# A 46,610-instruction transformer kernel: cross attention in a fixed order with other products between its steps, silu of the conditions kept in DRAM, index scores and root spreads a step later

## The chip, the cores and the metric

The kernel runs on one core of a Trainium2 chip. The metric is the device time of one execution in microseconds (us); smaller is better. Engine names: PE is TensorE (matmuls, weight loads are PEld), DVE is VectorE, ACT is ScalarE, POOL is GpSimd, SP is SyncE, which here only issues the transfers of weights.

## The reference, cut to what matters

Two blocks over a sequence of 256 rows of width 1024, all in fp32. The first block has two layers, each of a mixer (three kinds of attention, one of them with an index that selects keys), a cross attention to a memory of 256 rows, and a feed-forward network (FFN). The second has two layers over the latent rows and 256 rows of context, in which every norm is modulated by vectors that a condition gives.

```
def memory_cross_attention(hn, mem_n, w_q, w_kv, w_o):
    b, s, _ = hn.shape
    m = mem_n.shape[1]
    q = (hn @ w_q).reshape(b, s, H_X, HEAD_DIM)
    kv = (mem_n @ w_kv).reshape(b, m, 2, H_X, HEAD_DIM)
    sc = jnp.einsum('bqhd,bmhd->bhqm', q, kv[:, :, 0]).astype(jnp.float32) * HEAD_DIM ** -0.5
    p = jax.nn.softmax(sc, axis=-1).astype(hn.dtype)
    o = jnp.einsum('bhqm,bmhd->bqhd', p, kv[:, :, 1]).reshape(b, s, H_X * HEAD_DIM)
    return o @ w_o
...
        x = x + memory_cross_attention(rmsnorm(x, norm_cross[l]), mem_n, w_q_x[l], w_kv_x[l], w_o_x[l])
        x = x + swiglu(rmsnorm(x, norm_ffn[l]), w_gu[l], w_down[l])
...
def modulate(x, gain, shift, scale):
    return rms_norm(x, gain) * (1 + scale) + shift
...
        mod_l = (jax.nn.silu(c) @ w_mod[i] + b_mod[i]).reshape(b, N_MOD, 1, D_MODEL)
        mod_c = (jax.nn.silu(c_ctx) @ w_mod[i] + b_mod[i]).reshape(N_MOD, 1, D_MODEL)
...
    h = jnp.sin(freq * (h @ fw3 + fb3))
    h = (h @ fw4).astype(jnp.float32)
...
    h_fwd = h[:, :HY_WIDTH] * window
    h_bwd = h[:, HY_WIDTH:] * window
```

## The kernel before

Activations lie feature-major: x is [128 partitions, 8 chunks, rows], for the second block 512 columns wide, of which columns 0 to 255 are stream s=0 (latent rows) and 256 to 511 stream s=1 (context). Each fp32 product with a weight is made of three fp32r products (`mm3`, L300 to L302): high part by high part (`hh`, `whi`), low by high (`hl`, `whi`), high by low (`hh`, `wlo`). "A product" below is one of the three, 128x128 by 256 columns, unless a width is given. A weight tile of 128x1024 comes through SP's queue into one of four `raw` buffers; ACT casts it to `whi` (L195) and DVE makes `wlo` (L196). PSUM has two tags of four banks each, `acc` (products) and `aux` (everything else).

A main generator issues the products of the model in order; side generators (attention, index, norms) are advanced one step at each `yield` of the main one, so that the number of yields sets how many products stand between two steps. A scheduler then orders every engine's instructions by its own estimate of when inputs are ready. Each engine runs its list in order, so what stands in a list behind a waiting instruction waits too.

`cross(l)` makes q (tile `xq`, L905, on ACT), then for two pairs of heads: `scores` (L442; row maxima on DVE L450 and L454, exp on ACT L455 into `e`), `normalise` (DVE, L464 to L474), `flip` (transposes on PE, L489, copied by ACT to `pt`, L491), `values` (L501, split into `xoh` and `xol`, L308 and L309), then the products with w_o. Between its steps it advances a `fill`: for l = 0 keys and values of the memory for layer 1 (`mem_kv(1)`, tiles `xk1`, `xv1`), for l = 1 hyena's filter (`hyena_filter`: products with `w4` in two halves t, L1525 and L1526; DVE multiplies by a window to `hf` and `hb` and forms `hs`, L1529 to L1532; DFT products L1538 from `hs`).

`mods` makes the modulation vectors in the background, on DVE, from tiles `mraw` of w_mod and a broadcast `cb` of both conditions (1 MB, loaded five times; L1186), to which silu is applied each time (L1190 on ACT, L1191 on DVE). `norm2` makes the norms of the second block: sums of squares (`ssq`, L1281), the root on POOL (`nrs2`), a spread over the partitions (L1289), and `modulate`, for each of 8 chunks k: DVE L1290, ACT L1312, ACT L308 (`hh2`), DVE L309 (`hl2`). `fm2_split` starts a part with s=0 in an order with k outermost over four tiles of weights (96 products, 12 for each k), then s=1 tile by tile (24 products each, 3 for each k):

```
            if wide and not last:
                for k in range(KC):
                    for (wh, wl), p in zip(ws, ps):
                        self.mm3(p[:, ts], (wh[:, k], wl[:, k]), (xh[:, k, ts], xl[:, k, ts]), k == 0, k == KC - 1)
                    if k % 2:
                        yield
```

## Time and profile before

| | |
|---|---|
| Time, median of 3 runs | 2919.56 us (2919.30 to 2922.55) |
| Profiled execution: its own time, its span | 2920.18 us, 2918.4 us |
| PE busy | 2879.8 us (99%) |
| DVE, ACT, POOL busy | 2016.0 (69%), 1279.5 (44%), 73.2 us (3%) |
| Mean granted clock of PE | 0.994 of full speed |
| Transfers | 452.03 MB, 155 GB/s over the span |

The span is what the trace covers; the execution's own time has 1.8 us more. [...] A wait is put down to the instruction that released it ("<-").

### The profile page before, as it was taken

The numbers are of one execution on the slowest core, as the hardware profiler recorded it, in microseconds if no ns is written. First come the engines' busy times: TensorE is split into PE (matmuls) and PEld (weight loads), VectorE is DVE, ScalarE is ACT, GpSimd is POOL, SyncE is SP. The second block draws the span as 40 slices with busy tenths as digits, with TensorE's granted clock in tenths as the row PEclk, the third lists the DMA queues.
The fourth block names the chain that finished last, engine by engine and source line by source line (L and its number), as shares of the span: only waits on it lengthen the run. The fifth ranks groups of instructions, "written<-read, shape, count | busy, mean of one in ns | idle before, by whom it ended". The sixth has DMA issues, their size and how long they took to land.

```text
span 2918.4 us, 46610 instructions
## 1 busy us (share of the span) xinstructions
PE 2879.8 (99%) x18228; PEld 2535.0 (87%) x18228; DVE 2016.0 (69%) x3915; ACT 1279.5 (44%) x2017; POOL 73.2 (3%) x135
## 2 busy tenths in 40 slices
PE   8999999999999999999999999999999999999999
PEld 8899899989979988888977888888888889977999
DVE  7767798876878788875657656565787846535655
ACT  6665644577654542222425532123322225423543
POOL 0000000000000000000011000000000000000000
PEclk9999999999989999999999999999999999999999
DMA  7555577655546746564322234443465524522554
GB/s 228 161 162 165 176 232 237 187 155 161 181 157 208 223 147 188 185 182 124 105 67 80 88 118 146 144 148 102 139 190 184 183 92 136 164 72 87 160 185 147
DMA packets 150685, 452.03 MB, mean 155 GB/s; under 512 B 17151, under 2 KB 24872, under 8 KB 149696
## 3 DMA queue, kind: packets, MB, share of 16 engines
q1 hardware_dynamic: 147040, 435.94, 47.7%
q0 software_dynamic: 3280, 12.94, 1.4%
q8 instruction: 143, 2.34, 0.3%
q14 instruction: 78, 0.64, 0.1%
q10 hardware_dynamic: 144, 0.16, 0.0%
HBM read 447.93 MB, written 1.05 MB: 154 GB/s over the span
## 4 chain that ended last, share of the span: by engine, by line
PE 90%; issue 4%; DVE 3%; ACT 2%; DMA 1%; POOL 1%; POOLq 0%; ACTq 0%; DVEq 0%
PE acc L300 25%; PE acc L302 25%; PE acc L301 25%; PE acc L418 3%; PE acc L419 3%; PE acc L420 3%; PE aux L1857 1%; PE aux L442 1%; DVE wlo L196 1%; PE aux L489 1%; PE aux L501 1%; ACT whi L195 1%; PE aux L1552 0%; PE aux L1850 0%; PE aux L1569 0%
## 5 line engine op out<-in xcount | busy, mean ns | idle before, releaser
L195 ACT CAST whi<-raw 128x1024 fp32r<-128x1024 f32 x674 | 705.3, 1049 | 1334.9 <-PE acc L301 602.9
L300 PE MATMUL acc<-hh,whi 128*128 128x256 f32 (+1 forms) x3728 | 1174.7, 316 | 5.2 <-ACT hh L308 3.0
L196 DVE TENSOR_TENSOR wlo<-raw,whi 128x1024 fp32r<-128x1024 f32 x674 | 823.0, 1223 | 513.0 <-ACT whi L195 506.2
L302 PE MATMUL acc<-hh,wlo 128*128 128x256 f32 (+1 forms) x3728 | 1169.4, 314 | 0.1
L301 PE MATMUL acc<-hl,whi 128*128 128x256 f32 (+1 forms) x3728 | 1166.8, 313 | 0.2
L300 PEld LDWEIGHTS acc<-hh,whi 128*128 128x128 f32 x3728 | 701.0, 189 | 64.0 <-issue 8.7
L301 PEld LDWEIGHTS acc<-hl,whi 128*128 128x128 f32 x3728 | 703.3, 189 | 51.3 <-DVE hl L309 1.0
L302 PEld LDWEIGHTS acc<-hh,wlo 128*128 128x128 f32 x3728 | 702.2, 189 | 49.1 <-issue 0.4
L1200 DVE CUSTOM_DVE_ANT_0 mjunk<-mraw,cb 128x512 f32<-128x512 f32 x576 | 396.7, 689 | 26.8 <-DMA mraw<-w_mod 15.5
L300 PE MATMUL acc<-hidh,whi 128*128 128x256 f32 (+1 forms) x1152 | 373.3, 324 | 0.0
L302 PE MATMUL acc<-hidh,wlo 128*128 128x256 f32 (+1 forms) x1152 | 373.2, 324 | 0.0
L301 PE MATMUL acc<-hidl,whi 128*128 128x256 f32 (+1 forms) x1152 | 372.9, 324 | 0.0
L301 PEld LDWEIGHTS acc<-hidl,whi 128*128 128x128 f32 x1152 | 216.9, 188 | 20.0
L300 PEld LDWEIGHTS acc<-hidh,whi 128*128 128x128 f32 x1152 | 216.9, 188 | 20.0
L302 PEld LDWEIGHTS acc<-hidh,wlo 128*128 128x128 f32 x1152 | 216.9, 188 | 19.8
L418 PE MATMUL acc<-whi,hh 128*128 128x512 f32 x320 | 131.8, 412 | 0.0
L420 PE MATMUL acc<-wlo,hh 128*128 128x512 f32 x320 | 127.0, 397 | 0.0
L419 PE MATMUL acc<-whi,hl 128*128 128x512 f32 x320 | 126.6, 396 | 0.0
L1387 DVE TENSOR_TENSOR u<-acc,u 128x512 f32<-128x512 f32 (+1 forms) x88 | 55.0, 625 | 82.5 <-PE acc L302 81.8
L1367 DVE SCALAR_TENSOR_TENSOR x<-acc,modT,x 128x256 f32<-128x256 f32 x136 | 59.8, 478 | 49.3 <-PE acc L302 49.2
L418 PEld LDWEIGHTS acc<-whi,hh 128*128 128x128 f32 x320 | 60.2, 188 | 16.6 <-issue 3.5
L419 PEld LDWEIGHTS acc<-whi,hl 128*128 128x128 f32 x320 | 60.3, 188 | 14.7 <-issue 1.4
(368 smaller groups left out, 2651.6 us busy)
## 6 DMA issues: line engine op xcount, KB each, us to landing
mraw<-w_mod SPq DMA_DIRECT2D x288, 256.0 KB, 3.1
raw<-w_in SPq DMA_DIRECT2D x126, 512.0 KB, 3.6
raw<-w_gu SPq DMA_DIRECT2D x88, 512.0 KB, 4.2
raw<-ffn_a_in SPq DMA_DIRECT2D x88, 512.0 KB, 3.5
raw<-ffn_b_in SPq DMA_DIRECT2D x88, 512.0 KB, 3.5
raw<-ret_in SPq DMA_DIRECT2D x48, 512.0 KB, 3.5
raw<-w_down SPq DMA_DIRECT2D x44, 512.0 KB, 3.9
raw<-ffn_a_out SPq DMA_DIRECT2D x44, 512.0 KB, 3.5
```

The lines of the kernel that those rows point to most:

```text
L195: nc.scalar.copy(hi, raw)
L196: nc.vector.tensor_sub(lo, raw, hi.bitcast(F32))
L300: nc.tensor.matmul(out, wh, xh, start=first, stop=False)
L301: nc.tensor.matmul(out, wh, xl, start=False, stop=False)
L302: nc.tensor.matmul(out, wl, xh, start=False, stop=last)
L418: nc.tensor.matmul(o, xh[:, k, ts], wh[:, kk], start=first, stop=False)
L419: nc.tensor.matmul(o, xl[:, k, ts], wh[:, kk], start=False, stop=False)
L420: nc.tensor.matmul(o, xh[:, k, ts], wl[:, kk], start=False, stop=last)
L442: nc.tensor.matmul(banks[h][:, off[t]], pr.q[s, t * P:(t + 1) * P], pr.k[s, :nk], start=True, stop=True)
L1200: self.tc.keep_in_program_order(nc.vector.tensor_tensor_reduce(junk, w, cb[:, s, k * 512:(k + 1) * 512], 1.0, 0.0, ALU.mult, ALU.add, accu ...
L1367: nc.vector.scalar_tensor_tensor(xm, ps[:, ts], gate[:, s, m:m + 1], xm, ALU.mult, ALU.add)
L1387: nc.vector.tensor_tensor(u, pb, u, ALU.mult)
```

## The change

- `silu_c` makes silu of both conditions once, from a load `cc` at the start of the program, and writes it to DRAM; `mods` broadcasts that, and has no silu of its own.
- `cross` advances the fill once ahead of the products for q and again behind them, and then runs a written order of steps. `mem_kv(1)` and the filter yield at other places, the filter takes `acc` banks in place of `aux`. A small exp on a tile of ones stands behind q in the code, whose result nobody reads.
- `values_diff` issues its three products before the squares on them.
- `index` and `norm2` have one more `yield`.

```
         nc = self.nc
         k, v = self.xk[l], self.xv[l]
-        ps = self.fm_first([("w_kv", l, 0), ("w_kv", l, 1)], self.mem)
         if l == 0:
+            ps = self.fm_first([("w_kv", l, 0), ("w_kv", l, 1)], self.mem)
             self.mrs = self.norm_a(self.mpool)
+            yield
         else:
             for c in range(2):
-                nc.vector.tensor_tensor(k[:, c], ps[c], self.mrsb, ALU.mult)
-        yield
+                ps, = self.fm_first([("w_kv", l, c)], self.mem)
+                nc.vector.tensor_tensor(k[:, c], ps, self.mrsb, ALU.mult)
+                yield
...
+    def silu_c(self):
+
+        nc = self.nc
+        t = self.small.tile([P, 16], F32, name="ccs")
+        nc.scalar.activation(t, self.cc, AF.Sigmoid)
+        nc.vector.tensor_tensor(t, t, self.cc, ALU.mult)
+        self.silu = self.dram.tile([P, 16], F32, name="silu")
+        nc.gpsimd.dma_start(self.silu, t)
...
                 fill = self.hyena_filter()
+                next(fill)
+            ps = self.fm_first([("w_q", l, 0), ("w_q", l, 1)], (self.hh, self.hl))
+            q = mp.tile([P, 2, T], F32, name="xq")
+            for c in range(2):
+                nc.scalar.activation(q[:, c], ps[c], AF.Copy, scale=0.125)
+
+            nc.scalar.activation(self.small.tile([P, 1], F32, tag="exp0", name="exp0", bufs=1), self.ones, AF.Exp)
+            rs = self.norm_a()
+            yield
+            next(fill, None)
+            yield
...
-            for i, _ in enumerate(self.attention(pairs, lambda p: True)):
-                if i:
+            p0, p1 = pairs
+            for step in (lambda: (self.scores(p0), self.scores(p1)), None, None, lambda: (self.normalise(p0), self.flip(p0)),
+                         lambda: self.normalise(p1), None, lambda: self.flip(p1), lambda: self.values(p0), None, lambda: self.values(p1)):
+                if step:
+                    step()
+                else:
                     next(fill, None)
                 yield
...
+        if self.stop != "block1":
+            self.cc = self.small.tile([P, 16], F32, name="cc")
+            nc.gpsimd.dma_start(self.cc, bass.AP(tensor=a["cc"].tensor, offset=0, ap=[[16, P], [1, 16]]))
         lv = lt.tile([P, 2, 2, 2, 64], F32, name="lamv")
         nc.gpsimd.dma_start(lv, bass.AP(tensor=a["lamv"].tensor, offset=0, ap=[[0, P], [1, 512]]))
...
-        nc.gpsimd.dma_start(cb, bass.AP(tensor=a["cc"].tensor, offset=0, ap=[[0, P], [1, 2 * D]]))
+        nc.gpsimd.dma_start(cb.rearrange("p s d -> p (s d)"), self.silu.rearrange("(o p) k -> o (p k)", o=1).to_broadcast([P, 2 * D]))
         junk = pool.tile([P, D // 2], F32, name="mjunk")
-        for s in range(4):
-            c = cb[:, s // 2, (s % 2) * 512:(s % 2) * 512 + 512]
-            nc.scalar.activation(junk, c, AF.Sigmoid)
-            nc.vector.tensor_tensor(c, c, junk, ALU.mult)
...
         self.rsqrt(rs, v)
+        yield
         yield
...
-                pf, pb = self.aux(), self.aux()
+                pf, pb = self.acc(), self.acc()
...
-                    ps = self.aux()
+                    ps = self.acc()
```

Three places of the compiled order follow; line numbers differ by 3 to 27 between the two kernels (L905 is L927 after the change, L1289 is L1314).

ACT in the first cross attention, before: `mjunk<-cb` is the silu of the conditions, `whi` the cast of a weight tile, `e,sum` the exponentials.

```order
L1190 ACTIVATE mjunk<-cb 128x512
L195 CAST whi<-raw 128x1024 x2
L905 ACTIVATE xq<-acc 128x256 x2
L1190 ACTIVATE mjunk<-cb 128x512 x2
L455 ACT_TABLE_LOAD
L455 ACTIVATE e,sum<-aux,m,nrs 128x256 x7
L195 CAST whi<-raw 128x1024
L455 ACTIVATE e,sum<-aux,m,nrs 128x256
```

After the change, from the same two casts on:

```order
L195 CAST whi<-raw 128x1024 x2
L927 ACTIVATE xq<-acc 128x256 x2
L195 CAST whi<-raw 128x1024
L455 ACT_TABLE_LOAD
L455 ACTIVATE e,sum<-aux,m,nrs 128x256 x8
L195 CAST whi<-raw 128x1024 x2
```

The silu has left the list at this place, q follows the casts directly, and all eight exponentials stand together. The two small exps on ones, the sigmoid of `silu_c` and a table load for each of the two functions stand at the very start of ACT's list, ahead of the first high part of the memory (L312); on DVE the product of `silu_c` stands behind the two instructions on `lamv` (L1116, L1118), which already stood at its start, and all three are ahead of the first low part.

PE in the second cross attention, before, from the sums of squares behind the products for q; `sh` is the filter's hidden layer, the numbers tell tiles apart.

```order
L362 MATMUL aux_9795<-ones_70,ssq1_9793 128x1 x2
L442 MATMUL aux_9814<-xk1_88,xq_9790 128x256
...
L1525 MATMUL aux_9868<-w4_9861,sh_9194 128x512
L1526 MATMUL aux_9869<-w4_9861,sh_9194 128x512
L489 MATMUL aux_9884<-ident_69,e_9813 128x128
...
L1525 MATMUL aux_9898<-w4_9861,sh_9194 128x512
L1526 MATMUL aux_9899<-w4_9861,sh_9194 128x512
...
L1538 MATMUL aux_9921<-hs_9867,dft_9863 128x512
...
L489 MATMUL aux_9932<-ident_69,e_9834 128x128 x4
L1538 MATMUL aux_9939<-hs_9867,dft_9863 128x512 x2
```

After the change:

```order
L362 MATMUL aux_9822<-ones_72,ssq1_9820 128x1 x2
L1551 MATMUL acc_9829<-w4_9746,sh_9197 128x512
L1552 MATMUL acc_9830<-w4_9746,sh_9197 128x512
L442 MATMUL aux_9843<-xk1_90,xq_9815 128x256
...
L1551 MATMUL acc_9883<-w4_9746,sh_9197 128x512
L1552 MATMUL acc_9884<-w4_9746,sh_9197 128x512
L1564 MATMUL acc_9893<-hs_9752,dft_9748 128x512
L1564 MATMUL acc_9923<-hs_9752,dft_9748 128x512
L1564 MATMUL acc_9948<-hs_9752,dft_9748 128x512
L1564 MATMUL acc_9959<-hs_9752,dft_9748 128x512
L1564 MATMUL acc_9893<-hs_9752,dft_9748 128x512
L1564 MATMUL acc_9923<-hs_9752,dft_9748 128x512
L489 MATMUL aux_9903<-ident_71,e_9842 128x128 x4
```

The first half of the products with `w4` stands ahead of the scores, the second behind them, and six DFT products, four of them for t = 0 alone, ahead of the transposes.

DVE at this place after the change, behind the two low parts of weights; `m` are the row maxima:

```order
L1555 TENSOR_TENSOR hf<-acc,win 128x512
L1556 TENSOR_TENSOR hb<-acc,win 128x512
L450 TENSOR_REDUCE m<-aux 128x1
L1557 TENSOR_TENSOR hs<-hf,hb 128x512
L1558 TENSOR_TENSOR hs<-hf,hb 128x512
...
L1555 TENSOR_TENSOR hf<-acc,win 128x512
...
L1556 TENSOR_TENSOR hb<-acc,win 128x512
...
L450 TENSOR_REDUCE m<-aux 128x1 x2
...
L450 TENSOR_REDUCE m<-aux 128x1
L1557 TENSOR_TENSOR hs<-hf,hb 128x512
L454 TENSOR_SCALAR m<-m,nrs 128x1
L1558 TENSOR_TENSOR hs<-hf,hb 128x512
```

The second `hf`, `hb` and both second `hs` now stand among the row maxima, ahead of every `e<-e,rsum`; before, they stood behind the maxima and among those.

PE at the start of the even mixer before, `hidh2` being the end of the FFN ahead of it, `hh2` the new part's input:

```order
L1281 MATMUL aux_15227<-ones_70,ssq0_15085 128x1 x2
...
L1289 MATMUL aux_15264<-ident_69,nrs2_15231 128x128 x2
...
L300 MATMUL acc_15447<-hh2_9808,whi_15258 128x256
...
L1281 MATMUL aux_15415<-ones_70,ssq1_15083 128x1 x2
...
L1289 MATMUL aux_15475<-ident_69,nrs2_15419 128x128 x2
L300 MATMUL acc_15448<-hh2_9808,whi_15333 128x256
```

After the change:

```order
L1305 MATMUL aux_15216<-ones_72,ssq0_15074 128x1 x2
...
L1314 MATMUL aux_15283<-ident_71,nrs2_15220 128x128 x2
...
L300 MATMUL acc_15436<-hh2_9737,whi_15247 128x256
...
L1305 MATMUL aux_15404<-ones_72,ssq1_15072 128x1 x2
...
L1314 MATMUL aux_15488<-ident_71,nrs2_15408 128x128 x2
L300 MATMUL acc_15437<-hh2_9737,whi_15277 128x256
```

By the numbers of the rows 10 products stood between the first sums (`ssq0`) and their spread, and now 34; the spread for s=1 stood 51 products behind the first one that reads `hh2` (45 of s=0 left), and now 63 (33 left). Between `ssq1` and its spread stand 4 products, as before.

## Rows read from the trace of the kernel before

**Rows 1.** The page, part 1: busy time, share of the span, instructions.

```profile
PE 2879.8 (99%) x18228; PEld 2535.0 (87%) x18228; DVE 2016.0 (69%) x3915; ACT 1279.5 (44%) x2017; POOL 73.2 (3%) x135
```

**Rows 2.** Waits of PE over the span: us in total, times, longest.

```profile
PE aux L442 <- ACT xq L905: 4.9, 2, 3.3
PE aux L1525 <- ACT e L455: 3.0, 1, 3.0
PE aux L1289 <- POOL nrs L341: 2.8, 5, 1.0
PE aux L871 <- DVE ixt L728: 2.4, 2, 1.4
PE aux L521 <- ACT bo L522: 1.6, 2, 0.8
```

**Rows 3.** Timeline of ACT, first cross attention: start, duration, instruction, idle before.

```profile
309.23 0.63 ACT L1190 ACTIVATE mjunk<-cb 128x512 f32<-128x512 f32 x1 [6.61 <-DMA cb<-cc]
...
311.64 0.65 ACT L905 ACTIVATE xq<-acc 128x256 f32<-128x256 f32 x2
...
315.13 1.28 ACT L455 ACT_TABLE_LOAD   x1 [0.69 <-DVE m L454]
316.43 0.56 ACT L455 ACTIVATE e<-aux,m,nrs 128x256 f32<-128x256 f32 x1
```

**Rows 4.** Timeline of PE, first cross attention: its beginning, then the first FFN products.

```profile
305.92 0.50 PE L362 MATMUL aux<-ones,ssq 128*128 128x1 f32 x4
...
336.49 0.28 PE L300 MATMUL acc<-hh,whi 128*128 128x256 f32 x1
...
336.84 0.28 PE L300 MATMUL acc<-hh,whi 128*128 128x256 f32 x1
```

**Rows 5.** Stretches: us, busy PE, PEld, DVE, ACT, POOL; PEclk; DMA share; GB/s.

```profile
310.80:317.60 6.80, 5.53 (x24) 4.36 (x25) 6.02 (x14) 5.09 (x11) 0.65 (x1) 0.50 0.45 154
809.10:826.20 17.10, 13.80 (x32) 5.28 (x28) 11.75 (x35) 6.95 (x19) 0.00 (x0) 0.50 0.27 91
50.00:55.00 5.00, 3.56 (x34) 3.17 (x34) 5.00 (x12) 3.36 (x5) 0.00 (x0) 1.00 0.39 120
2430.50:2433.90 3.40, 3.40 (x17) 3.38 (x16) 3.23 (x18) 2.60 (x6) 0.00 (x0) 0.50 0.00 0
```

**Rows 6.** Timeline of PE, second cross attention: its beginning, w4, first FFN product.

```profile
805.96 0.50 PE L362 MATMUL aux<-ones,ssq 128*128 128x1 f32 x4
...
813.78 2.07 PE L1525 MATMUL aux<-w,sh 64*128 64x512 f32 x2 [3.05 <-ACT e L455]
...
840.90 0.28 PE L300 MATMUL acc<-hh,whi 128*128 128x256 f32 x1
```

**Rows 7.** Timeline of DVE in the second cross attention.

```profile
806.77 2.37 DVE L196 TENSOR_TENSOR wlo<-raw,whi 128x1024 fp32r<-128x1024 f32 x2
809.18 0.76 DVE L450 TENSOR_REDUCE m<-aux 128x1 f32<-128x256 f32 x2
...
815.89 0.69 DVE L1529 TENSOR_TENSOR hf<-aux,win 128x512 f32<-128x512 f32 x1 [1.16 <-PE aux L1525]
...
818.46 0.69 DVE L1531 TENSOR_TENSOR hs<-hf,hb 128x512 f32<-128x512 f32 x1
```

**Rows 8.** Timelines of PE and DVE at the start of the even mixer.

```profile
1412.99 0.71 PE L1289 MATMUL aux<-ident,nrs 128*128 128x128 f32 x4 [0.53 <-POOL nrs L341]
...
1421.21 0.38 PE L301 MATMUL acc<-hl,whi 128*128 128x256 f32 x1
...
1420.73 0.76 DVE L309 TENSOR_TENSOR hl<-modh,hh 128x256 fp32r<-128x256 f32 x2
```

**Rows 9.** Timeline of DVE at the start of the retention.

```profile
2425.68 0.17 DVE L1749 TENSOR_SCALAR lge<-lg 128x8 f32<-128x8 f32 x1 [2.78 <-DMA lg<-logit]
```

**Rows 10.** Timelines of POOL and DVE at the start of the program.

```profile
1.29 0.77 POOL L1114 DMA_DIRECT2D lamv<-lamv  x1 [0.41 <-issue]
...
7.35 0.42 DVE L1116 TENSOR_TENSOR lamp<-lamv 128x256 f32<-128x256 f32 x1 [2.35 <-DMA lamv<-lamv]
```

## The prediction

> **What bounds the kernel.** I read the page first: PE is busy 99% of the span, DVE 69%, ACT 44% [rows 1]. So only what PE waits for can be won, and what runs on it at half clock. Next came the list of PE's waits [rows 2]: those that the change touches are 4.9 us on q's copy, 3.0 us ahead of the filter's `w4` products, 2.8 us on the roots of five norms, 2.4 us on the index, 1.6 us on the squares of `values_diff`. Then the granted clock: it is 0.50 for 6.8 us of the first cross attention and 17.1 us of the second, where PE is busy 5.53 and 13.80 us [rows 5]; work at half clock takes twice its time, so that half of these, 2.8 and 6.9 us, are lost beside the waits. A measurement of this kernel can tell about 0.2%, 5.8 us, from no change.

> **First cross attention.** From its beginning at 305.92 to the first FFN product at 336.49 it takes 30.57 us [rows 4]. Of that 3.3 is the wait on q [rows 2] and 2.8 the clock, which leaves 24.5. The wait arises on ACT: its list has the silu of `cb` ahead of two casts and q, and ACT stood 6.61 us until the transfer of `cb` had landed, at 309.23; q ran at 311.64 [rows 3]. With the silu gone ACT starts the casts when PE leaves the buffers, and q is done at about 308.3, 2.3 us behind the beginning: in the second cross attention, where no silu stands ahead of it, PE's wait for it ended 2.1 us behind, 0.5 us of sums [rows 6] and 1.6 of wait [rows 2]. PE has 24 products on the memory until then, a product being 0.12 us (three from 336.49 to 336.84 [rows 4]): to 309.2. So the scores no longer wait. What is late next is the softmax: a table load of 1.28 and eight exponentials of 0.56 us [rows 3], pitch 0.55, behind maxima that now stand behind one more low part of a weight, 1.2 us each (two take 2.37 [rows 7]). Worked through in the order of the list, the first table load ends at 313.7, the last exponential of the first pair at 315.9, its normalised `e` at 317.0 to 317.8. PE has scores (2 us), 24 products on keys and 24 on values until 316.7: a wait of about half a us. The second pair's last `e` comes behind two more low parts at 321.9, with PE there at 321.1: another half. With a few tenths for the last split of `xoh` I put 0.9 us on top of 24.5: 25.4, a gain of 5.2. None of these waits is as long as that on the index, 1.4 us [rows 2], around which the clock stayed 1.00 [rows 5], so I expect full clock. Bounds: 2.5 if the softmax is 2.7 us later, 7.6 if the small waits inside the 24.5 go too.

> **Second cross attention.** From 805.96 to 840.90 are 34.94 us [rows 6]. Its waits are again 1.6, 4.9 less 3.3, and 3.0 us [rows 2]; with 6.9 for the clock 23.4 is left. Now two products with `w4`, 0.93 us each at full clock (two took 2.07 at half clock [rows 6]; a tenth of that is drain), fill the time until q, and the scores run from 808.3 to 810.2 without a wait. The next two end at 812.05; `acc` banks are free for them, so the 3.0 us wait on an `aux` bank is gone. Then come four DFT products for t = 0, whose `hs` DVE made at 812.05, in the list order: low parts to 809.14 [rows 7], `hf` and `hb` 0.69, a maximum 0.42 (two are 0.76), `hs` twice 0.69 [rows 7]. They need banks that `hf` and `hb` of t = 1 set free, at 814.3 and 815.4. They end at 816.3. The next needs `hs` of t = 1: it stands on DVE behind all eight maxima, the last four of which wait for exponentials that begin only behind the first `hs` and the table load, so at 813.6. I get 817.6 for it: PE waits 1.3 us there and some 0.6 before. The transposes then find `e` within 0.3 us. 23.4 and 2.8 for all waits (half a us is for hand-overs that I don't see) give 26.2, a gain of 8.7. Bounds: 11.5 without any wait; 2 if the `hs` wait is 4.6 us, as the waits of before together, and half clock follows it.

> [...]

> **Silu of the conditions once.** 20 sigmoids on ACT and 20 products on DVE go (each 0.63 to 0.69 us [rows 3, 7]); apart from the place above, both engines have slack there, so I cost it at nothing: the cover is PE's own work, and without it at most the idle of ACT behind the other four loads of `cb` would show, which no wait of PE names. At the start it costs: POOL issues `cc` ahead of `lamv`, 0.77 us [rows 10], and DVE's first low part stands behind what waits for `lamv`, at 7.35 [rows 10], and now behind the silu too. PE's third product needs a low part, and PE is the bound from there on: 0.8 us lost. Bounds 0 (`lamv` lands no later) and 2.5 (ACT's list stands until `cc` lands, as late as `lamv`). The table load for it on ACT runs while inputs are in flight. The two small exps are at the start too, so the table load in front of the softmax stays: nothing gained, nothing lost.

> **values_diff.** The second and third product no longer wait for a square: 1.6 us at two places [rows 2], 1.5 gained; 0 if the squares are then late for the transposes.

> **Index.** In PE's list the first scores stay behind the same 72 products, only the second ones move by 24. The wait is in front of the first: 2.4 us stay, gain 0 (bounds 0 and 2.4).

> **Root spreads.** For s=0 the spread had no wait, and moves 24 products, 2.8 us. For s=1 there are still 4 products between sums and spread at three of four starts, so the waits of 0.5 [rows 8] stay. But the spread itself is now 12 products nearer to the first use of its stream. Before, the last two `hl` were made from 1420.73 on, the first of them done about 1421.15, and the product that reads it ran at 1421.21 with 0.38 in place of 0.28 us [rows 8]: no slack at all. The modulation takes 8.2 us from the spread, paced by ACT, whatever PE does. So 12 products, 1.4 us, become waits of PE, at the start of the even mixer and of the next FFN. At the FFN behind the even mixer the spread has 25 products behind its sums, which saves 0.4, but is 20 nearer to the use: 2.3 less 0.4, 1.9. At the retention DVE stands until 2425.68 for a transfer [rows 9], well behind the spread, and what follows hangs on that: 0. Together 4.7 lost. Bounds: 0, and 14.9 as below.

> **Sum.** The profiled execution took 2920.18 us, 0.6 above the median of 2919.56. 0.8 and 4.7 lost, 1.5, 5.2 and 8.7 gained: 9.9 gained. 2919.56 less 9.9 is **2909.7 us**.

> **Rivals.**
> 1. *The later spreads cost nothing*: the modulation would have to run faster once ACT and DVE are less loaded there. For it: nothing but that it is worked out from an order. Against it: the missing slack of [rows 8]. 4.7 less: 2905.0.
> 2. *The wait for `hs` is the new wait of the second cross attention*: `hs` of t = 1 comes some us later than I get, through eight maxima in DVE's list, each waiting for ACT, and the clock goes to half again. For it: the chain was as long before, when it held up `w4` at 813.78 [rows 6]. Price 3 us of wait and 2 to 3.4 of clock: 2914.7 to 2916.
> 3. *Half clock at the starts of parts, so that it ends slower*: each new stall of 1.4 us at the spreads could bring half clock, as the retention's start had it for 3.4 us [rows 5]. At 6.8 us, as in the first cross attention, each costs 3.4 more: 14.9 with the stalls at three starts, and the sum is a loss of 0.3. It decides for slower, by more than 5.8 us, from 8.7 us of loss to the clock at each of three starts, which is the whole 17.1 us stretch of the second cross attention [rows 5] at each: 2925.3. Against it: the waits of 1.4 us on the index left the clock at 1.00 [rows 5].
> 4. *The crosses give less than half*, because the written order only moves the waits behind other work: 7 us less, 2916.7.

> **Chances.** The forecast 0.46, rival 1 0.15, rivals 2 and 4 together 0.30, rival 3 0.09. The first two are faster by more than 5.8 us, and a small part of rivals 2 and 4; so faster 0.63, within 0.2% 0.28, slower 0.09. The range leaves out rival 3 and the outer part of rival 1: 2903 to 2917.5.

> **What would show it.** Right: q's wait gone from PE's list at both crosses, first FFN products 25 and 26 us behind the beginning, one wait of about a us on `hs`, clock 1.00 at both; a few waits on `hh` or `hl` at 1.4 us together behind the spread of s=1 at the two starts, 1.9 at the third. The `values_diff` wait gone, the index one still there. Wrong: half clock at 815 to 825 (rival 2), no wait behind the spreads (rival 1), half clock there (rival 3), or a first product at 9 us instead of 8 and more waits until 30 us.

## The result, and the profile after

| kernel | median, us | runs |
|---|---|---|
| before | 2920.88 | 4 (2919.30 to 2922.55) |
| after | 2889.22 | 4 (2887.65 to 2892.57) |

The ratio is 0.9893 (95% interval 0.9882 to 0.9905): 31.7 us faster, where 9.9 were forecast and the range ended at 2903. The direction was right and the size was not. The profiled execution after took 2887.65 us, its span is 2885.7.

The page's part 1 of after, which answers to [rows 1]:

```profile
PE 2855.2 (99%) x18228; PEld 2523.8 (87%) x18228; DVE 2001.3 (69%) x3896; ACT 1270.0 (44%) x2002; POOL 77.9 (3%) x137
```

PE runs the same 18228 products and is busy 24.6 us less. Some 9 of that is the half clock that is gone, an estimate: in before a 256-column product's pitch, from one start to the next, was 0.213 us at 0.50 (316.16 to 317.44) and 0.117 at 1.00 (317.65 to 318.94), and 16 scores took 3.79 us at 0.50 in before and 2.00 at 1.00 in after, so that 45 to 47% of 5.53 and of 13.80 [rows 5] are lost, where the prediction took half. Most of the other 15 to 16 us lie in how fast products run at full clock, as the experiments show, and this the prediction never looked at.

PE's waits in after (us in total, times, longest), which answer to [rows 2]:

```profile
PE acc L300 <- ACT hh L308: 3.7, 3, 1.9
...
PE aux L1314 <- POOL nrs L341: 2.6, 4, 1.0
PE aux L886 <- DVE ixt L731: 2.1, 2, 1.1
PE acc L301 <- DVE meml L313: 1.4, 1, 1.4
...
PE aux L533 <- DVE bo L526: 1.4, 2, 0.7
```

The 4.9 us on q and the 3.0 ahead of `w4` are gone. Windows of the two crosses, columns as in [rows 5]:

```profile
300.00:328.00 28.00, 27.03 (x226) 24.57 (x225) 20.31 (x48) 18.41 (x40) 0.71 (x1) 1.00 0.55 190
...
790.00:818.00 28.00, 26.89 (x155) 18.01 (x153) 20.07 (x50) 17.63 (x40) 1.28 (x2) 1.00 0.48 171
```

The granted clock is 1.00 in both, against 0.50 for 6.8 and 17.1 us before [rows 5]. The marks of PE's timeline: the first spread of the program, then each cross from its sums to the first FFN product behind it, which answer to [rows 4, 6].

```profile
22.85 0.71 PE L374 MATMUL aux<-ident,nrs 128*128 128x128 f32 x4 [0.54 <-POOL nrs L341]
...
303.02 0.50 PE L362 MATMUL aux<-ones,ssq 128*128 128x1 f32 x4
...
306.30 2.00 PE L442 MATMUL aux<-xk,xq 64*128 64x256 f32 x16
...
327.80 0.28 PE L300 MATMUL acc<-hh,whi 128*128 128x256 f32 x1
...
793.22 0.50 PE L362 MATMUL aux<-ones,ssq 128*128 128x1 f32 x4
...
817.88 0.28 PE L300 MATMUL acc<-hh,whi 128*128 128x256 f32 x1
```

In before the first of these marks stands at 21.37. Stage by stage, before less after, is (the last column is of the run `same_addresses`, told below):

| stretch | before to after | the edits alone |
|---|---|---|
| start to the first spread | -1.5 | -2.6 |
| on to the first cross | +4.4 | +2.5 |
| first cross | 30.57 to 24.78: +5.8 | 24.99: +5.6 |
| between the crosses | +4.05 | +1.3 |
| second cross | 34.94 to 24.66: +10.3 | 24.64: +10.3 |
| to the end of the span | +9.7 | +2.0 |

Each column is read from one trace of a kernel. In the four traces with the old start the first spread lies between 20.98 and 21.79, and in the twelve with the new one (cc_behind, whose start differs, apart) between 21.91 and 24.16, so that a difference of a us at the start tells little.

The crosses give 16.1 us, where 13.9 were forecast. Some 18 us come from the stretches between and behind them, in which 1.5 were to be won and 4.7 lost.

### The profile page after: what moved, and what is told of

Read it like the earlier page. It is cut to its first block, busy times and chain, and to the rows that moved or that the text cites. A ratio compares the mean times of both kernels' runs of the same rounds, so it can differ in the third digit from the quotient of the medians.

```text
span 2885.7 us, 46572 instructions
## 1 busy us (share of the span) xinstructions
PE 2855.2 (99%) x18228; PEld 2523.8 (87%) x18228; DVE 2001.3 (69%) x3896; ACT 1270.0 (44%) x2002; POOL 77.9 (3%) x137
## 4 chain that ended last, share of the span: by engine, by line
PE 85%; issue 3%; DVE 2%; ACT 1%; POOL 0%; DMA 0%; POOLq 0%; DVEq 0%; ACTq 0%
PE acc L301 25%; PE acc L300 25%; PE acc L302 25%; PE acc L418 2%; PE acc L419 2%; PE acc L420 2%; PE aux L1883 1%; PE aux L489 1%; PE aux L501 1%; PE aux L1578 0%; PE aux L1876 0%; PE aux L442 0%; DVE wlo L196 0%; PE aux L1595 0%; DMA lg<-logit 0%
## 5 line engine op out<-in xcount | busy, mean ns | idle before, releaser
L300 PE MATMUL acc<-hh,whi 128*128 128x256 f32 (+1 forms) x3728 | 1167.7, 315 | 5.0 <-ACT hh L308 3.7
L301 PE MATMUL acc<-hl,whi 128*128 128x256 f32 (+1 forms) x3728 | 1166.5, 314 | 0.1
L302 PE MATMUL acc<-hh,wlo 128*128 128x256 f32 (+1 forms) x3728 | 1164.5, 314 | 0.0
L300 PEld LDWEIGHTS acc<-hh,whi 128*128 128x128 f32 x3728 | 699.1, 188 | 66.1 <-issue 7.7
L301 PEld LDWEIGHTS acc<-hl,whi 128*128 128x128 f32 x3728 | 701.7, 188 | 50.3 <-issue 0.8
L302 PEld LDWEIGHTS acc<-hh,wlo 128*128 128x128 f32 x3728 | 699.9, 188 | 46.6 <-issue 0.4
L302 PE MATMUL acc<-hidh,wlo 128*128 128x256 f32 (+1 forms) x1152 | 370.4, 322 | 0.0
L301 PE MATMUL acc<-hidl,whi 128*128 128x256 f32 (+1 forms) x1152 | 370.3, 321 | 0.0
L300 PE MATMUL acc<-hidh,whi 128*128 128x256 f32 (+1 forms) x1152 | 368.8, 320 | 0.0
L301 PEld LDWEIGHTS acc<-hidl,whi 128*128 128x128 f32 x1152 | 216.3, 188 | 18.5
L300 PEld LDWEIGHTS acc<-hidh,whi 128*128 128x128 f32 x1152 | 216.3, 188 | 18.5
L302 PEld LDWEIGHTS acc<-hidh,wlo 128*128 128x128 f32 x1152 | 216.1, 188 | 16.6
```

Source lines behind the costliest of these rows:

```text
L300: nc.tensor.matmul(out, wh, xh, start=first, stop=False)
L301: nc.tensor.matmul(out, wh, xl, start=False, stop=False)
L302: nc.tensor.matmul(out, wl, xh, start=False, stop=last)
```

## The experiments

In all of them "left" means `hh`, `hl` of block 1 and `hidh`, `hidl`, which lie on the side of SBUF on which the pool `small` stands, and "right" `hh2`, `hl2`. The change adds three tiles to `small`: `cc` and `ccs` of 64 bytes and `exp0` of 32 bytes a partition. All that lies above moves by 160 bytes: `hh` and `hidh2` from address 91936 to 92096, that is from 32 to 192 modulo 256. `hh2` stays at 196576, 224 modulo 256. Of a product's two inputs "the moving operand" means the activation (`hh`, `hl` and the like); the other is a 128x128 piece of a weight tile, which PEld loads for the product (a LDWEIGHTS of 128x128, 189 ns at L300 in the page of before). The weight tiles themselves stay at the same addresses in all runs. A pad is a small tile that is set to zero once and never read.

**pad_before and pad_after**: 32 bytes ahead of the left side, in before and in after.

```diff
             self.small = ep(name="small", bufs=1)
+            nc.gpsimd.memset(ep(name="pad", bufs=1).tile([P, 8], F32, name="pad"), 0.0)
```

> The kernel before with one unused 32-byte tile per partition behind the pool of small tiles: every instruction keeps its place on PE, DVE, ACT and SP, only the addresses of hh, hl, hidh, hidl, hidh2, hidl2 and the other activations of the left side move by 32 bytes, from 32 to 0 modulo 64, which is what the change's new small tiles did by their 160 bytes. Theory 1 (a product runs faster when its moving operand begins at a multiple of 64 bytes): the pitch of 512-column products on hidh2 and hidl2 falls from 234.2 ns to 227 to 230, that of 256-column products on hidh from 117.2 to 115.8, the time falls by 9 to 13 us, to 2908 to 2911. Theory 2 (the products of the changed kernel are faster because ACT and DVE do less, or because the instructions stand in another order): all pitches as before, time within 2 us of the kernel before.

Measured 2906.65 us, ratio 0.9956 (0.9940 to 0.9973).

> The changed kernel with the same unused 32 bytes: the same operands go back to 32 modulo 64, with no instruction moved on PE, DVE or ACT. Theory 1: the pitch on hidh2 and hidl2 goes back to 234, the time rises by 9 to 13 us over the changed kernel, to 2898 to 2902. Theory 2: as the changed kernel, 2889 within 2.

Measured 2910.50, ratio 0.9967 (0.9954 to 0.9980). 32 unused bytes make before 14 us faster and after 21 us slower, with the compiled order of PE, DVE and ACT unchanged. So addresses cost as much as the change.

Theory 2 is refuted by both, but theory 1 doesn't hold as it was written either. In pad_before the 512-column products on `hidh2`, `hidl2` gained only 1 ns (234.3 to 233.3 ns from one start to the next, where 227 to 230 were expected), and the time was won on the 256-column products on `hh`, `hl` (118.1 to 114.2).

**both_aligned**: after, with 32 bytes behind `hl2`, so that the right side too is at 192 modulo 256.

```diff
         self.hl2 = cp.tile([P, KC, 2 * T], F32R, name="hl2")
+        nc.gpsimd.memset(cp.tile([P, 8], F32, name="pad2"), 0.0)
```

> The changed kernel with 32 unused bytes at the end of the right side, so that hh2 and hl2, the input of every part of the second block, begin at a multiple of 64 bytes too (both stood at 32 modulo 64 in both kernels). Theory 1: their 512-column products fall from a mean of 233.3 ns to about 229, 3160 of them, some 13 us, and the 256-column ones from 120 to about 118, 3200 of them, some 5 us: the time falls by 12 to 20 us, to 2869 to 2877. Theory 2: 2889 within 2.

Measured 2865.68, ratio 0.9811 (0.9796 to 0.9826): 23.5 us below after.

**same_addresses and before_shifted** close the square: the edits at before's addresses, and before at after's.

```diff
# same_addresses, on after: a right-side pool "early", closed ahead of setup2()
-            self.cc = self.small.tile([P, 16], F32, name="cc")
+            self.cc = self.earlyp.tile([P, 16], F32, name="cc")
...
# before_shifted, on before: 160 bytes
+            nc.gpsimd.memset(ep(name="pad", bufs=1).tile([P, 40], F32, name="pad"), 0.0)
```

`ccs` and `exp0` move likewise; one of the two small exps is left out, and each other tile has the address it has in before.

> The changed kernel with its three new small tiles in a pool of their own on the right side that is closed before the second block's pools open, so that all 158 names of the kernel before have exactly the addresses of before; PE, DVE, POOL and SP have the order of the changed kernel, ACT has one of the two small exps less. By the terms measured so far (start 1.4 lost, crosses 16.1 gained, values_diff and smaller waits 1 to 3 gained, spreads 0): 2902 to 2905. By the sum on record, which had 4.7 lost at the spreads: 2909.7 and above. If addresses play no part in the changed kernel: 2889.

Measured 2901.69 (2900.85 to 2903.72), ratio 0.9937 (0.9925 to 0.9950).

> The kernel before with 160 unused bytes behind the small tiles, so that all operands of the left side have exactly the addresses of the changed kernel, and no instruction of PE, DVE, ACT or SP moves. If addresses and edits add: 12 to 16 us less than the kernel before, 2905 to 2909, and this and the kernel with the edits alone together make up the 31.7 us. If addresses only help the changed kernel's order: 2920.

Measured 2909.45 (2908.49 to 2911.45), ratio 0.9964 (0.9950 to 0.9977). Before is 2920.7 beside these two: the edits alone give 19.0, the addresses alone 11.3, together 30.3 of the 31.7; the rest of 1.4 is not resolved. In before_shifted PE, DVE, ACT and SP have the same lists as in before; POOL has the zeroing of the pad more.

Where the addresses show is in the duration of a product. PE by line and shape (total us, mean ns of one), the FFN's second product of block 2, 512 columns, first before:

```profile
L302 PE MATMUL acc<-hidh,wlo 128*128 128x512 f32 x432 | 171.3, 396 | 0.0
L300 PE MATMUL acc<-hidh,whi 128*128 128x512 f32 x432 | 171.2, 396 | 0.0
L301 PE MATMUL acc<-hidl,whi 128*128 128x512 f32 x432 | 171.2, 396 | 0.0
```

before_shifted, where only addresses differ:

```profile
L301 PE MATMUL acc<-hidl,whi 128*128 128x512 f32 x432 | 170.2, 394 | 0.0
L300 PE MATMUL acc<-hidh,whi 128*128 128x512 f32 x432 | 169.4, 392 | 0.0
L302 PE MATMUL acc<-hidh,wlo 128*128 128x512 f32 x432 | 167.7, 388 | 0.0
```

and after:

```profile
L302 PE MATMUL acc<-hidh,wlo 128*128 128x512 f32 x432 | 169.7, 393 | 0.0
L301 PE MATMUL acc<-hidl,whi 128*128 128x512 f32 x432 | 169.6, 392 | 0.0
L300 PE MATMUL acc<-hidh,whi 128*128 128x512 f32 x432 | 168.0, 389 | 0.0
```

In same_addresses the three rows read as in before, 396 each. A duration of 396 ns overlaps the next product's, which starts 234 ns behind in before, so the price is the pitch, from one start to the next, at full clock. From the trace's starts (gaps of 222 to 242 ns with 512 columns, of 105 to 130 with 256, so that waits drop out) three products took 702.8 ns in before and 686.9 in before_shifted: 15.9 less, 432 times, 6.9 us. The same sum for the 256-column products of block 1 gives 1.9 (`hidh`, `hidl`, 5.5 ns some 350 times) and 2.3 (`hh`, `hl`, 1.5 ns some 1540 times): 11.1 of the 11.3 measured. The first of the three terms is the firm one: the 512-column pitch on `hidh2`, `hidl2` is the same within 0.1 ns in all four kernels that have them at 32, and in all six that have them at 192. The term of `hidh` is not firm: its 256-column products in block 1 took 115.6 ns in after and 117.8 in cc_behind, at the same addresses. For both_aligned against after it gives 13.9 (13.2 ns, 1056 times) and 9.4 (8.8 ns, some 1070 times) on `hh2`, `hl2`: 23.3 of 23.5.

**residue_0, residue_128, residue_96_160 and hh2_only**: after, with pads of other sizes (16 and 56 words, 48 and 24, 40 and 16; in hh2_only 24 words between `hh2` and `hl2`).

> The changed kernel with unused bytes on both sides, so that hh, hl, hidh2, hidl2, hh2 and hl2 begin at 0 modulo 256 (in the changed kernel 192 on the left side, 224 on the right). Theory 1a (a multiple of 64 is all that counts): pitches as in the kernel with both sides aligned, time 2866 within 4. Theory 1b (the place within 256 bytes counts: so far 256-column products took 114.0 ns at 64, 117.6 at 192, 118.1 at 32, 120.3 at 224, and 512-column ones 233.3 at 64, 228.8 at 192, 234.3 at 32, 233.4 at 224): pitches of its own here, which differ from 117.6 and 228.8 by more than 1 ns, and a time more than 5 us from 2866, either way. Theory 2 (address is not the cause): 2889.

Measured 2899.06, ratio 0.9924 (0.9909 to 0.9939).

> As the kernel with 0 modulo 256, with the same operands at 128 modulo 256, the residue of the weight tiles whi and wlo themselves. Theory 1a: 2866 within 4. Theory 1b: pitches of its own again. If what counts is the distance of the moving operand from the weights, this is the extreme case, best or worst of the five.

Measured 2876.90, ratio 0.9848 (0.9834 to 0.9863). Neither of the two is at 2866, so that theory 1a is refuted: a multiple of 64 is not all that counts.

> The changed kernel with the left side's operands at 96 and the right side's at 160 modulo 256, the two residues not yet seen at multiples of 32: if being a multiple of 64 is a part of it, 512-column products on hidh2 (96) and hh2 (160) take 233 to 235 ns, 256-column ones on hh (96) 118 to 120; if only the place within 256 counts and 128 is its best, those at 160 are near 227 and those at 96 too.

Measured 2894.84 in one run.

> The changed kernel with 96 unused bytes between hh2 and hl2: hh2 goes to 128 modulo 256, hl2 stays at 224. If a product's pitch is set by the address of its own moving operand: 512-column products on hh2 about 227 ns (L300 and L302), on hl2 233.5 (L301) as before. If it is set by the two together or by the place in the instruction stream: all three move alike, or none.

Measured 2875.64 in one run.

Mean pitch in ns, by the moving operands' address modulo 256 (the residue), over the three products of a triple (high, low, high part of the input): with 512 columns those of `hidh2`, `hidl2` and of `hh2`, `hl2`, which agree within 0.1 in all kernels with the residue; with 256 those of block 1's `hh`, `hl` (at 160, of `hh2`, `hl2`).

| residue | 0 | 32 | 64 | 96 | 128 | 160 | 192 | 224 |
|---|---|---|---|---|---|---|---|---|
| 512 columns | 232.7 | 234.3 | 233.3 | 233.3 | 226.7 | 233.3 | 228.9 | 233.3 |
| 256 columns | 118.8 | 117.7 to 118.3 | 114.1 to 116.3 | 118.3 | 119.8 | 116.8 | 117.5 to 117.6 | 119.9 |

In hh2_only `hh2` is at 128 and `hl2` at 224. If each product had the pitch of its own operand, a triple would have a mean of 228.9 (twice 226.7 and 233.3); it has 231.1 (232.5 and 228.9 for the two on `hh2`, 232.0 for the one on `hl2`). With 256 columns the triple has 117.9, below the 119.9 or 119.8 that it has with both operands at 224 or both at 128. So a product's pitch is not set by its own operand alone, and what else sets it stays open.

The table can be read off rows. Timeline of PE, first and last of 20 products in a row, in before:

```profile
1254.72 0.40 PE L302 MATMUL acc<-hidh,wlo 128*128 128x512 f32 x1
...
1259.17 0.40 PE L300 MATMUL acc<-hidh,whi 128*128 128x512 f32 x1
```

and in residue_128:

```profile
1244.65 0.39 PE L302 MATMUL acc<-hidh,wlo 128*128 128x512 f32 x1
...
1248.95 0.39 PE L300 MATMUL acc<-hidh,whi 128*128 128x512 f32 x1
```

4.45 us are 19 pitches of 234.2 ns, 4.30 us 19 of 226.3; the granted clock is 1.00 around both.

**cross_alone and silu_alone**: before with `mem_kv`, `cross` and `hyena_filter` of after; before with `lambdas`, `mods` and `silu_c` of after (and a pad that keeps the left side at 32 modulo 256).

> The kernel before with only the new cross attention (its order, mem_kv and the filter's yields and banks), with the silu of the conditions still made in the background, the small exp left out and all addresses as before. Theory 1 (the second cross attention gains by its order alone, the first one needs the silu gone from ACT's list): the second takes 24 to 26 us in place of 34.9, the first keeps a wait of 2 to 3.4 us on q and takes 27 to 29 in place of 30.6; time 2907 to 2911. Rival (order alone is enough in both): both about 24.7 us, time 2903 to 2906. As recorded, by the pitch nothing is added here, since no address moves.

Measured 2908.36, ratio 0.9960 (0.9945 to 0.9975).

> The kernel before with only the silu of the conditions made once and kept in DRAM, and 128 unused bytes behind the small tiles, so that hh, hl, hidh2 and hidl2 keep their address modulo 256. Theory 1 (the first cross attention needs the silu gone from ACT's list, and the early load of the conditions delays the start): PE's wait on q in the first cross attention falls from 3.3 to under 1 us, the half clock there goes, it takes 25 to 28 us in place of 30.6; the start is 1.3 to 1.5 us later, as in the changed kernel; nothing else moves: time 2916 to 2920 by the start and the first cross attention. Rival (the order of steps made the first cross attention shorter): it stays at 29 to 31 us, time 2920 to 2923.

Measured 2915.25, ratio 0.9980 (0.9970 to 0.9990), a little below the range. Between the marks the first cross takes 29.56 us in cross_alone and 25.27 in silu_alone, the second 24.64 and 35.42. In the three traces with the old order and the silu in place (before, before_shifted, pad_before) the first takes 29.7 to 32.4. So the first cross is won by taking the silu off ACT's list, the second by the written order and the `acc` banks together; no run tells these two apart. In cross_alone PE still waits for q in the first cross, and in silu_alone it doesn't, as their timelines show:

```profile
311.88 3.56 PE L442 MATMUL aux<-xk,xq 64*128 64x256 f32 x16 [2.24 <-ACT xq L914]
```

```profile
311.19 2.00 PE L442 MATMUL aux<-xk,xq 64*128 64x256 f32 x16
```

**after_spread_back**: after without the second `yield` of the norms.

```diff
         self.rsqrt(rs, v)
         yield
-        yield
```

> The changed kernel without the second yield in norm2, so that the roots are spread where they were; no address moves. The prediction on record: the later spread costs 4.7 us of new waits, so that this kernel is 4.7 us faster than the changed one, 2884.5. Theory now (the scheduler put products of a second weight tile between the late chunks of the first one, so that no wait arose): the wait of 0.4 us at one start comes back, otherwise nothing, 2889 within 1.5.

Measured 2888.77, ratio 0.9887 (0.9871 to 0.9904), after being 2889.22: the later spreads cost nothing that these runs can tell, and not the 4.7 that were forecast.

**cc_behind**: after, with `cc` loaded behind `lamv`.

> The changed kernel with the load of the conditions issued behind that of lamv in POOL's list. Theory (lamv's later landing delays DVE's first low part): the third product on the memory, at 11.14 us in the changed kernel and at 9.81 before, is 0.6 to 1.3 us earlier, 9.8 to 10.5. Rival (ACT's list, which stands until the conditions have landed, is what delays it): at 11 us or later.

Measured 2888.98 in one run. The third product starts at 9.95, as the theory has it, and the first spread comes at 21.45 instead of 22.85; 1.4 us cannot be told in the time. The run doesn't settle which list was the cause, since the scheduler changed both: DVE goes on from `lamv` at 7.46 instead of 8.60, and ACT makes its first two high parts at 5.05, ahead of the sigmoid, instead of standing for `cc` until 6.63. The third product is a high by high one there, where it was high by low.

**best and best2**: after with pads for 128 modulo 256 in block 2, left and right, and 64 in block 1 (32 words ahead, 24 behind `hl2`, 16 ahead of block 2; in best2 96 words ahead).

> The changed kernel with three unused pieces, so that the operands of the first block (hh, hl) begin at 64 modulo 256, where 256-column products took 114.0 ns, and those of the second block (hh2, hl2, hidh2, hidl2) at 128, where 512-column products took 226.7 ns. If the residue alone sets the pitch: block 1 as fast as in the kernel before with 32 bytes, plus the crosses, block 2 as in the kernel with 128 (2043 us from the end of the second cross attention): 2848 to 2860 us. If the two kernels' pitches hang on something else that went along with the pads: 2866 to 2889.

Measured 2860.08, ratio 0.9785 (0.9769 to 0.9802).

> The best kernel so far with its left side 256 bytes further on: hh at 64 modulo 256 as there, but at 320 modulo 512, as in the kernel before with 32 bytes, where 256-column products took 114.0 ns against 116.3 ns in the best one; block 2 stays at 128. If the residue modulo 512 (or more) counts: hh back at 114 to 115, 2848 to 2855. If not: 116.3 again, 2860 within 4.

Measured 2858.10 (2855.84 to 2863.25), ratio 0.9790 (0.9776 to 0.9803). Best ended at the upper edge of its range, and the two can't be told apart. Block 1's `hh` and `hl` ran at 116.3 and 115.2 ns, not at the 114.1 of pad_before, whose addresses have the same residue; and at 32 the kernels with equal addresses, before, cross_alone and same_addresses, have 118.1, 117.7 and 118.3. So for 256 columns the residue does not say all.

## Why the prediction was wrong

**The missing term: where operands lie, 11.3 us.** The sum priced each edit by its instructions and took every product at one pitch ("a product being 0.12 us"). The step "silu of the conditions once", put at nothing but for the start, counted its instructions and not its tiles. The 160 bytes of those, and of the exps' tile, moved the left operands, and their products run 0.4 to 2.3% faster. before_shifted shows this without any edit. So more than a third of the gain was luck: the added bytes happened to be good ones, and with 32 more pad_after is 21 us slower.

**The root spreads, forecast -4.7, measured nothing.** This is the step that failed within the sum. Rival 1, a chance of 0.15, had the outcome right but not the reason: the modulation did not run faster (the last `hl` begin 7.72 us behind the spread below, 7.74 in [rows 8]). "The spread itself is now 12 products nearer to the first use of its stream" counted only the products of s=0 between them (45 before, 33 now) and took those of s=1 to stand as before. The order of after at that place (PE; `acc_15436` and `acc_15437` belong to two weight tiles):

```
9444 L300 MATMUL acc_15436<-hh2_9737,whi_15247 128x256
9445 L301 MATMUL acc_15437<-hl2_9738,whi_15277 128x256
9446 L302 MATMUL acc_15437<-hh2_9737,wlo_15278 128x256
9447 L300 MATMUL acc_15437<-hh2_9737,whi_15277 128x256
9448 L301 MATMUL acc_15437<-hl2_9738,whi_15277 128x256
9449 L301 MATMUL acc_15436<-hl2_9738,whi_15247 128x256
```

Before, the eight chunks of one tile stood in a row, and the last was read first by product 67 behind the spread (45 and 22). Now products of the second tile on early chunks stand between the late chunks of the first, and the last is read first by product 66 (33 and 33). The scheduler gave back 11 of the 12. The timelines of PE and DVE in after, which answer to [rows 8]:

```profile
1387.51 0.71 PE L1314 MATMUL aux<-ident,nrs 128*128 128x128 f32 x4 [0.53 <-POOL nrs L341]
...
1395.61 0.49 PE L301 MATMUL acc<-hl,whi 128*128 128x256 f32 x2
```

```profile
1395.23 0.76 DVE L309 TENSOR_TENSOR hl<-modh,hh 128x256 fp32r<-128x256 f32 x2
```

PE has no wait up to the last `hl`, although 8.1 us lie between spread and `hl`, as reckoned. "Paced by ACT, whatever PE does" was right (ACT has no wait from 1388.71 to the last `hh`, done at 1395.51); what PE does in that time was not looked at. At the FFN behind the even mixer the 1.9 us did not come either: PE waits for neither `hh` nor `hl` there, and the wait of 0.44 us for the roots is gone. At the retention, where I put 0, the wait for `hh` is longer than in before, first before, then after:

```profile
2427.98 0.38 PE L300 MATMUL acc<-hh,whi 128*128 128x256 f32 x1 [0.69 <-ACT hh L308]
```

```profile
2396.10 0.38 PE L300 MATMUL acc<-hh,whi 128*128 128x256 f32 x1 [1.39 <-ACT hh L308]
```

In after_spread_back it is 0.83, which the time doesn't show.

**The crosses, 5.2 and 8.7 forecast, 5.6 and 10.3 from the edits.** The mechanism held: q leaves the silu's shadow, the scores no longer wait, the `aux` bank's 3.0 us go, the clock stays. The terms were mis-sized by the small waits that I added: 0.9 and 2.8 us were put on top of 24.5 and 23.4, and 0.5 and 1.2 came (0.2 to 0.3 and 0.5 to 0.8, if 45 to 47% went to the half clock and not half). (By the working's own figures for the first cross, half a us, 0.8 and a few tenths, it should have been some 1.5 and not 0.9.) In the first cross PE waits 0.81 us in one place:

```profile
314.97 1.46 PE L489 MATMUL aux<-ident,e 128*128 128x128 f32 x8 [0.81 <-DVE e L470]
```

In the second I put 2.8 for all waits; the timeline of PE shows one on `hs`, 11.1 us behind the beginning (reckoned: 11.6):

```profile
799.01 1.98 PE L1564 MATMUL acc<-hs,dft 128*128 128x512 f32 x4
801.15 2.37 PE L1564 MATMUL acc<-hs,dft 128*128 128x512 f32 x4 [0.16 <-DVE hf L1555]
804.36 1.98 PE L1564 MATMUL acc<-hs,dft 128*128 128x512 f32 x4 [0.83 <-DVE hs L1557]
```

Rivals 2 and 4 are refuted by these rows. Rival 3 is too: at the starts of the even mixer (1375 to 1400 us) and of the two FFNs behind it (1635 to 1665, 2005 to 2030) the clock is 1.00 in after. At the retention's start it falls as it did before the change (0.50 from 2430.5 to 2433.9 [rows 5]), in after behind waits of 1.39 and 0.33 us on `hh`, in before behind 0.69 and 0.33:

```profile
2397.00:2400.50 3.50, 3.17 (x18) 3.11 (x18) 3.43 (x18) 3.38 (x9) 0.00 (x0) 0.65 0.00 0
```

The price at which rival 3 decides for slower was summed wrongly: 8.7 us lost at each of three starts would have given 2935.8, and 5.2 are enough for 2925.3.

The longest pause at the crosses of after was 0.83 us, and the clock stayed 1.00. In cross_alone 2.24 us are left on q in the first cross; the 16 scores behind them took 3.56 us, and 2.00 in silu_alone, where PE doesn't wait there, and the granted clock from 305 to 340 us was 0.95 and 1.00. The products in cross_alone last 0.28 us again from 315.58 on. How long a pause has to be for half clock to follow it was not shown.

**The start, forecast -0.8, measured -1.5 in after and -2.6 in same_addresses.** In after this lies between the 0.8 and the bound of 2.5 us lost; in same_addresses it is at that bound. ACT's list did stand for `cc`: 2.40 us, and its first high part of the memory, behind the sigmoid in the list, began at 6.75. `lamv` behind it came 1.25 us later than the 7.35 of [rows 10], where only the 0.77 of its later issue were reckoned, and PE's second product waited for the low part behind it:

```profile
6.63 0.22 ACT L854 ACTIVATE ccs<-cc 128x16 f32<-128x16 f32 x1 [2.40 <-DMA cc<-cc]
```

```profile
8.60 0.43 DVE L1143 TENSOR_TENSOR lamp<-lamv 128x256 f32<-128x256 f32 x1 [3.66 <-DMA lamv<-lamv]
```

```profile
10.01 0.58 PE L301 MATMUL acc<-meml,whi 128*128 128x256 f32 x1 [1.39 <-DVE meml L313]
```

**values_diff and the index, forecast 1.5.** The 1.6 us on the squares at L521 [rows 2] and 0.7 at the transposes (L532, after the change L533) became 0.5 on `pt` and 1.4. PE's waits there, first before, then after:

```profile
PE aux L532 <- DVE bo L525: 0.7, 2, 0.4
```

```profile
PE aux L521 <- ACT pt L491: 0.5, 2, 0.3
```

What the squares no longer hold up, the next step does, a net 0.4. The index kept 2.1 of its 2.4 us. From the first spread to the first cross the edits gained 2.5 us, and between the crosses 1.3; PE's waits fell by 1.8 us in the first of these stretches (5.6 to 3.8; the first mixer's transposes no longer wait 1.0 us for `e`) and by 0.6 in the second (2.4 to 1.8). Which edit took them away, and where the 2.0 us behind the second cross come from, was not tested.

In sum the edits gave 19.0 against 9.9: 4.7 of the difference is the spreads, 2.0 the crosses, and the rest small gains that no run tells apart, less a dearer start.

## What to carry to other kernels

When a change adds or resizes a tile, compare the addresses of the large operands in both kernels, and hold them fixed (a pool that is closed early, or a pad) before a gain is put down to an edit. Where products run at two speeds at one clock, try a few pads: 2858.1 us here, 31 below after, for 544 unused bytes a partition. For a step that is moved, count the products up to the first use in the whole new order, on both sides of the step, since a scheduler fills behind it with other work.

## What was not expected of the hardware

At the program's start the granted clock is recorded as 1.00 from 8 to 15 us in before, yet the products there last 0.41 us, as in the stretch at 0.50 behind 2430.5, and 0.28 from 13.85 on:

```profile
13.42 0.41 PE L300 MATMUL acc<-memh,whi 128*128 128x256 f32 x1
...
14.09 0.28 PE L301 MATMUL acc<-meml,whi 128*128 128x256 f32 x1
```

```profile
2432.43 0.41 PE L301 MATMUL acc<-hl,whi 128*128 128x256 f32 x1
```

In after the record has 0.56 from 8 to 14 us, with the same 0.41 us a product. So in before the first microseconds of the record don't tell the clock.
